# Storing the first output tile of an RMS-norm matmul in 60 and 68 rows, and the next three as one

## The chip, the cores and the metric

The kernel runs on one core of one Trainium2 chip. The metric is the device time of one execution in microseconds: 208.53 us, the median of three runs (208.49 to 208.7). Every instruction time below comes from one further execution, recorded by the hardware profiler.

## What is computed

```
x: 16 x 1024 x 512, float32     gamma: 512     weight: 512 x 768, float32
rms    = sqrt(mean(x**2, axis=-1, keepdims=True) + eps)
output = matmul(x / rms * gamma, weight)        # 16 x 1024 x 768, float32
```

## The kernel before

The 16384 rows of x are cut into 128 tiles of 128 rows (`NT`, L122). For each tile, ScalarE (ACT) squares and sums the rows (L197) and takes the root; VectorE (DVE) makes the reciprocal (L204). GpSimd (POOL) casts x to bf16 (L189, and L260 for the last four tiles of each 16). TensorE (PE) transposes the tiles two features at a time as 32-bit words (L231), and DVE copies them back (L240); the tiles of L260 are turned by DVE itself (L271). Then PE multiplies a tile with the weights in four steps of 128 features, each one product of 512 and one of 256 columns (L300). The sum in PSUM is scaled by the reciprocal root into an output buffer `ot`: even tiles by ACT (L279), odd ones by DVE (L281), in `finish_tile`. The weights are multiplied by gamma once, at the start.

No layer decides the order: the kernel writes its operations down in order, and `Order.emit` sends each to its engine with the waits that its reads and writes ask for.

Three kinds of transfers use the 16 DMA engines, from two queues:

- The queue of SyncE (SP; q1 in the profile) first gets the loads of tiles 0 to 31 and the weights: x in 4 tiles, the weights in two halves, x in 4, 8, 8 and 8 tiles. Then it gets all 22 stores of the output, each issued by SP when its last tile has been scaled.
- The queue of ACT (q10) gets gamma (512 numbers, as two rows) at the start, and later twelve loads of 8 tiles of x.

`stretches` (L128) says how the tiles of x and of the output are grouped into transfers. An output store usually covers a group of `OG` = 8 tiles; the first group has stores of 1, 1, 2 and 4 tiles, the last but one of 4 and 4, the last of 4, 2 and 2 (L139). There are four `ot` buffers of 8 tiles, used in turn. `rows` (L141) gives a transfer's place in memory: partition p of a group of t tiles holds the t rows p*t to p*t + t - 1, so that the part of a partition in a store is one stretch of memory: 3072 bytes for one tile, 6144 for two, 24576 for eight. In the first 8 tiles of the output the groups are of 4 tiles, so tiles 0, 1 to 3 and their parts lie at offsets within a stretch of 4 rows.

`store` (L288) is called after every tile and issues the transfer behind the last tile of its group. After the last one the program ends when the stores have landed.

Of the kernel before, what the change touches and what calls it, by code (L numbers as in the profile page):

```python
# [16 lines left out]
P = 128  # L17
# [83 lines left out]
def kernel(  # L101
# [9 lines left out]
    PE, DVE, ACT, POOL, SP = nc.tensor, nc.vector, nc.scalar, nc.gpsimd, nc.sync  # L111
    order = Order(tc)
# [5 lines left out]
    out = out.flatten_outer_dims()  # L118
# [5 lines left out]
    XG, OG = 16, 8  # L124
# [3 lines left out]
    def stretches(group, parts):  # L128
        first, size, i = {}, {}, 0
        for g in range(NT // group):  # L130
            for n in parts.get(g, [group]):
                for t in range(i, i + n):
                    first[t], size[t] = i, n
                i += n
        return first, size

    last = NT // OG - 1
    x_first, x_size = stretches(OG, {0: [4, 4]})
    o_first, o_size = stretches(OG, {0: [1, 1, 2, 4], last - 1: [4, 4], last: [4, 2, 2]})  # L139

    def rows(ap, i, n):  # L141
        base, t = (i - i % OG, OG) if OG <= i < XG else (x_first[i], x_size[i]) if i < OG else (i - i % XG, XG) if i < 2 * XG else (i - i % (2 * XG), 2 * XG)
        return ap[base * P:(base + t) * P, :].rearrange("(p t) d -> p t d", t=t)[:, i - base:i - base + n, :]

    def sb(name, shape, dtype):
        return nc.alloc_sbuf_tensor(name, shape, dtype).ap()
# [11 lines left out]
    ot = [sb(f"ot{n}", [P, OG, O], F32) for n in range(OTS)]  # L158
# [10 lines left out]
    def cells(name, slot, i, n=1):  # L169
        return [(name, slot, t) for t in range(i, i + n)]  # L170
# [114 lines left out]
    def accumulator():  # L285
        return next(turns) % 3

    def store(i):  # L288
        first, n = o_first[i], o_size[i]
        s = first // OG % OTS  # L290
        if i == first + n - 1:
            src = ot[s][:, first % OG:first % OG + n, :]
            order.transfer(SP, lambda: SP.dma_start(out=rows(out, first, n), in_=src), reads=cells("ot", s, first % OG, n))

    def hold(lhsT, of):
        run(PE, lambda: PE.ldweights(lhsT), of)  # L296
# [20 lines left out]
    def finish_tile(i, a, engine):  # L317
        s = i // OG % OTS

        before = [("ot", s, i % OG - 1)] if i == o_first[i] + o_size[i] - 1 else []  # L320
        scale(engine, ot[s][:, i % OG, :], ops[a][:, :O], rstd[:, i:i + 1],
              [("ops", a, 0), ("ops", a, 1), ("rstd", i)] + before, [("ot", s, i % OG)] + (opening if i == OG * (OTS - 1) else []))
        store(i)
# [158 lines left out]
```

## Time and profile before

| | |
|---|---|
| median of three runs | 208.53 us (208.49 to 208.7) |
| the profiled execution | 209.87 us |
| its span, first to last instruction | 207.9 us |
| granted PE clock, mean | 0.985 |
| moved by the DMA engines | 85.62 MB, mean 412 GB/s |
| read from / written to HBM | 35.13 MB / 50.33 MB |

How to read the lines that follow in the prediction. Of the page, the first line gives each engine's busy time, its share of the span and its instructions. The line that begins with DMA cuts the span into 40 slices of 5.2 us; each digit is the mean busy share of the 16 DMA engines in tenths. The lines that begin with q1 and q10 give the packets of a queue, its MB, and its packets' time as a share of 16 engines' span. A packet is what one engine moves in one piece; a store or load of 128 partitions makes a packet for each partition, and each engine that took part adds one of 4 bytes that raises the semaphore. The chain follows the work that ended last back from the last instruction. A line of the waits gives who waited for whom: total us, times, longest. A line of the windows gives a stretch in us, its length, the busy us of PE, weight loads, DVE, ACT and POOL with their instructions, the granted clock, the DMA share and the GB/s.

SP's issues of the first stores, from its timeline: two from 12.88 us to 14.69 (tiles 0 and 1), one at 17.20 (tiles 2 and 3), and one at 24.39 (tiles 4 to 7). The last scaling is that of tile 127 on DVE, from 197.96 for 1.02 us, and the last store is issued at 199.3.

### The profile page before, as it was taken

The numbers are of one execution on the slowest core, as the hardware profiler recorded it, in microseconds if no ns is written. First come the engines' busy times: TensorE is split into PE (matmuls) and PEld (weight loads), VectorE is DVE, ScalarE is ACT, GpSimd is POOL, SyncE is SP. The second block draws the span as 40 slices with busy tenths as digits, with TensorE's granted clock in tenths as the row PEclk, the third lists the DMA queues.
The fourth block names the chain that finished last, engine by engine and source line by source line (L and its number), as shares of the span: only waits on it lengthen the run. The fifth ranks groups of instructions, "written<-read, shape, count | busy, mean of one in ns | idle before, by whom it ended". The sixth has DMA issues, their size and how long they took to land.

```text
span 207.9 us, 2754 instructions
## 1 busy us (share of the span) xinstructions
PE 194.0 (93%) x1212; PEld 72.8 (35%) x717; DVE 149.4 (72%) x255; ACT 144.5 (70%) x343; POOL 60.0 (29%) x34
## 2 busy tenths in 40 slices
PE   7799999999999999999999999999999999999900
PEld 0244433443443334433443334443433334343300
DVE  0446557998589966998579966998579966999310
ACT  2698898877777686877777686777777686763300
POOL 1437651154206250154306060150703306000000
PEclk9999999999999999999999999999999999999995
DMA  5999999999999999999999999999999999999991
GB/s 207 426 433 448 378 418 430 421 439 418 440 419 432 429 429 435 430 427 426 435 421 421 441 427 432 432 427 418 426 440 419 440 435 424 430 423 426 421 394 58
DMA packets 5920, 85.62 MB, mean 412 GB/s; under 512 B 658, under 2 KB 660, under 8 KB 1556
## 3 DMA queue, kind: packets, MB, share of 16 engines
q1 hardware_dynamic: 4176, 60.29, 68.6%
q10 hardware_dynamic: 1732, 25.17, 28.4%
q8 instruction: 7, 0.11, 0.2%
q14 instruction: 5, 0.04, 0.0%
HBM read 35.13 MB, written 50.33 MB: 411 GB/s over the span
## 4 chain that ended last, share of the span: by engine, by line
PE 90%; DMA 2%; DVE 1%; issue 1%; ACT 1%; SPq 0%
PE ps L300 80%; PE ps L231 10%; DMA xt<-in_x_dram 2%; DVE ot L281 0%; ACT jk L197 0%; DVE xT L240 0%; DVE w_bf L281 0%; ACT ssq L202 0%; DVE rstd L204 0%; SPq L477 0%; SPq L436 0%
## 5 line engine op out<-in xcount | busy, mean ns | idle before, releaser
L300 PE MATMUL ps<-w_bf,xT 128*128 128x256 bf16 (+1 forms) x783 | 145.4, 326 | 1.1 <-DVE w_bf L281 0.2
L279 ACT ACTIVATE ot<-ps,rstd 128x768 f32<-128x768 f32 x64 | 57.6, 900 | 46.7 <-PE ps L300 46.5
L197 ACT ACTIVATE jk<-xt 128x512 bf16<-128x512 f32 x128 | 78.7, 618 | 3.1 <-DMA xt<-in_x_dram 3.1
L189 POOL CAST xb<-xt 128x2048 bf16<-128x2048 f32 (+3 forms) x21 | 46.4, 2218 | 110.0 <-DMA xt<-in_x_dram 57.6
L281 DVE TENSOR_SCALAR ot<-ps,rstd 128x768 f32<-128x768 f32 x64 | 64.8, 1013 | 9.7 <-PE ps L300 9.2
L296 PEld LDWEIGHTS <-xT 128*128 128x128 bf16 x400 | 39.3, 98 | 59.6 <-issue 58.2
L231 PE MATMUL ps<-ident_f,xb 128*128 128x128 f32 x200 | 54.4, 276 | 1.1 <-POOL xb L189 1.1
L240 DVE COPY xT<-ps 128x1024 bf16<-128x1024 bf16 (+1 forms) x53 | 34.6, 654 | 26.0 <-PE ps L231 25.2
L271 DVE STREAM_TRANSPOSE xTq<-xq 32x256 f32<-32x256 f32 x112 | 48.7, 435 | 1.9
L231 PEld LDWEIGHTS ps<-ident_f,xb 128*128 128x128 f32 x200 | 28.2, 143 | 46.4 <-issue 43.6
L300 PE MATMUL ps<-w_bf,xTq 128*128 128x256 bf16 (+1 forms) x217 | 41.8, 324 | 0.4
L197 ACT ACTIVATION_READ_ACCUMULATOR jk<-xt 128x1 f32 x128 | 24.3, 189 | 0.0
L296 PEld LDWEIGHTS <-xTq 128*128 128x128 bf16 x112 | 11.0, 98 | 14.5 <-issue 14.5
L260 POOL CAST xq<-xt 128x2048 bf16<-128x2048 f32 x7 | 13.3, 1894 | 4.2 <-DVE xTq L271 4.2
L204 DVE RECIPROCAL rstd<-ssq 128x8 f32<-128x8 f32 (+3 forms) x20 | 3.8, 192 | 7.1 <-ACT ssq L202 6.9
L202 ACT ACTIVATE ssq<-ssq,eps_sb 128x8 f32<-128x8 f32 (+3 forms) x20 | 6.0, 300 | 0.7
L300 PE MATMUL ps<-ot 128*128 128x512 bf16 x10 | 4.8, 628 | 1.4 <-DVE eps_sb L354 1.4
L279 ACT ACTIVATE w_bf<-ot,g_sb 128x768 bf16<-128x768 f32 x2 | 1.9, 936 | 1.1 <-DMA ot<-in_weight_dram 1.1
L377 DVE COPY g_sb<-ps 128x4 f32<-128x4 f32 x1 | 0.2, 161 | 3.2 <-PE ps L371 3.2
L341 ACT ACT_TABLE_LOAD x1 | 1.3, 1283 | 1.5 <-SPq L436 1.5
L281 DVE TENSOR_SCALAR w_bf<-ot,g_sb 128x512 bf16<-128x512 f32 (+2 forms) x3 | 1.4, 483 | 0.6 <-DMA ot<-in_weight_dram 0.6
L371 PEld LDWEIGHTS ps<-ident_f,ot 2*128 2x128 f32 x2 | 0.3, 200 | 2.6 <-issue 2.6
(10 smaller groups left out, 2.0 us busy)
## 6 DMA issues: line engine op xcount, KB each, us to landing
out_dram<-ot SPq DMA_DIRECT2D x13, 3072.0 KB, 22.9
xt<-in_x_dram ACTq DMA_DIRECT2D x12, 2048.0 KB, 20.0
xt<-in_x_dram SPq DMA_DIRECT2D x3, 2048.0 KB, 18.3
out_dram<-ot SPq DMA_DIRECT2D x4, 1536.0 KB, 11.9
out_dram<-ot SPq DMA_DIRECT2D x3, 768.0 KB, 8.8
xt<-in_x_dram SPq DMA_DIRECT2D x2, 1024.0 KB, 7.3
ot<-in_weight_dram SPq DMA_DIRECT2D x2, 768.0 KB, 7.0
out_dram<-ot SPq DMA_DIRECT2D x2, 384.0 KB, 21.0
```

Source lines behind the costliest of these rows:

```text
L189: run(POOL, lambda: POOL.tensor_copy(out=xb[s][:, i % 8:i % 8 + n, :], in_=src), of, cells("xb", s, i % 8, n))
L197: run(ACT, lambda: ACT.activation(out=jk[n], in_=src[:, 0, :], func=AF.Square, accum_out=ssq[:, i:i + 1]), of, [("jk", n), ("ssq", i)])
L202: run(ACT, lambda: ACT.activation(out=ssq[:, s], in_=ssq[:, s], func=AF.Sqrt, scale=1.0 / D, bias=eps_sb), [("ssq", t) for t in range(i, i ...
L204: run(DVE, lambda: DVE.reciprocal(out=rstd[:, s], in_=ssq[:, s]), [("rms", i)], [("rstd", t) for t in range(i, i + n)])
L231: run(PE, lambda: PE.transpose(out=tp[b][:, t, h, :], in_=words[:, lo:lo + P], identity=ident_f), cells("xb", s, j % 4 * 2 + t) + ["ident" ...
L240: run(DVE, lambda: DVE.tensor_copy(out=dst[:, t:t + n, :], in_=src[:, t:t + n, :]), [("tp", b)], cells("xT", j % XTS, t, n))
L260: run(POOL, lambda: POOL.tensor_copy(out=xq, in_=src), of, ["xq"])
L271: run(DVE, lambda: DVE.transpose(out=dst, in_=src), ["xq"], [("xTq", n)])
L279: run(ACT, lambda: ACT.mul(out=dst, in_=src, mul=r), reads, writes)
L281: run(DVE, lambda: DVE.tensor_single_scalar(out=dst, in_=src, scalar=r, op=mybir.AluOpType.mult), reads, writes)
L296: run(PE, lambda: PE.ldweights(lhsT), of)
L300: run(PE, lambda: PE.add_instruction(mybir.InstMatmult(name=nc.get_next_instruction_name(), engine=mybir.EngineType.PE, ins=[PE.lower_ap(r ...
```

## The change

The output's first group is stored as tile 0, tiles 1 to 3, and tiles 4 to 7. The store of tile 0 is issued as two transfers, one behind the other, of partitions 0 to 59 and 60 to 127. So there are still four transfers in the group. On the engines other than SP no instruction is added, taken away or moved.

```diff
-    o_first, o_size = stretches(OG, {0: [1, 1, 2, 4], last - 1: [4, 4], last: [4, 2, 2]})
+    o_first, o_size = stretches(OG, {0: [1, 3, 4], last - 1: [4, 4], last: [4, 2, 2]})
...
+    DIVIDED = (0,)
+    PARTS = [slice(60), slice(60, P)]
+
     def store(i):
         first, n = o_first[i], o_size[i]
         s = first // OG % OTS
         if i == first + n - 1:
-            src = ot[s][:, first % OG:first % OG + n, :]
-            order.transfer(SP, lambda: SP.dma_start(out=rows(out, first, n), in_=src), reads=cells("ot", s, first % OG, n))
+            src, dst = ot[s][:, first % OG:first % OG + n, :], rows(out, first, n)
+            for part in PARTS if first in DIVIDED else [slice(0, P)]:
+                store_rows(dst[part], src[part], cells("ot", s, first % OG, n))
+
+    def store_rows(dst, src, of):
+        order.transfer(SP, lambda: SP.dma_start(out=dst, in_=src), reads=of)
```

## The prediction

> **What bounds the kernel now.** I read the page first, then the windows of the tail, then the packet records of the trace. Two things on the page look like the bound at once:
>
> ```profile
> PE 194.0 (93%) x1212; PEld 72.8 (35%) x717; DVE 149.4 (72%) x255; ACT 144.5 (70%) x343; POOL 60.0 (29%) x34
> ...
> DMA  5999999999999999999999999999999999999991
> ...
> q1 hardware_dynamic: 4176, 60.29, 68.6%
> q10 hardware_dynamic: 1732, 25.17, 28.4%
> ...
> PE 90%; DMA 2%; DVE 1%; issue 1%; ACT 1%; SPq 0%
> ```
>
> The chain of work gives 90% to PE, but it stops where an instruction stops: at the last eviction (DVE L281, 197.96 to 198.98 us). The span runs on to 207.9. What lies between is one wait in the list of SP's own waits, beside the windows of the tail (the columns: stretch, its length, five engines, PE clock, DMA share, GB/s):
>
> ```profile
> SPq L477 <- DMA out_dram<-ot: 7.3, 1, 7.3
> ```
>
> ```profile
> 190.00:198.00 8.00, 7.87 (x49) 2.25 (x23) 3.98 (x7) 2.70 (x3) 0.00 (x0) 1.00 1.00 422
> 198.00:202.00 4.00, 0.00 (x0) 0.00 (x0) 0.98 (x1) 0.00 (x0) 0.00 (x0) 0.98 0.97 407
> 202.00:203.00 1.00, 0.00 (x0) 0.00 (x0) 0.00 (x0) 0.00 (x0) 0.00 (x0) 0.50 0.68 283
> 203.00:204.00 1.00, 0.00 (x0) 0.00 (x0) 0.00 (x0) 0.00 (x0) 0.00 (x0) 0.50 0.25 104
> 204.00:205.00 1.00, 0.00 (x0) 0.00 (x0) 0.00 (x0) 0.00 (x0) 0.00 (x0) 0.50 0.19 80
> 205.00:206.00 1.00, 0.00 (x0) 0.00 (x0) 0.00 (x0) 0.00 (x0) 0.00 (x0) 0.50 0.10 43
> 206.00:207.00 1.00, 0.00 (x0) 0.00 (x0) 0.00 (x0) 0.00 (x0) 0.00 (x0) 0.50 0.03 12
> ```
>
> The reader is to see that the 16 DMA engines are full to about 202 us and then do not stop together: a share of 0.19 is three engines of 16, and 0.10 is 1.6. The packet records (start, duration, bytes and queue; no engine number) say how. In a backlog each packet starts 3 to 4 ns before the previous one on its engine ends, and store and load packets alternate while both queues have work, so the 16 sequences can be strung together again. From 3.5 to 192 us no engine has an idle stretch that matters. The last store lands on 13 engines between 202.2 and 203.6 us, on two at 205.36 and 205.45, and on the last at 206.68. I call these three Z, Y and X. X, Y and Z are never short of packets; five of the quick engines are, for 0.04 to 0.63 us at 194.7, waiting for the next store. So the end is the work of one DMA engine, added up from the start of the run, and PE is not late for it: the last store is issued at 199.3, and X begins its first packet of it only at 204.82.
>
> **The change, part by part.** The number of stores stays 22, and SP's issues too (0.33 us each). Tile 0 goes out at the same place, behind the x loads in the same queue, whose packets last until 26.1 us on the first engine that gets through them, so its second issue (14.4 us at the latest) is covered by 11 us. The store of tiles 1 to 3 takes the place of the old one of tiles 2 and 3, issued at 17.20, covered by 9 us; tile 1 leaves at 17.20 and not at 14.4, into a queue that has not come to it. No wait is added that anything stands behind, and SP computes nothing. The output buffers are reused four groups later and the waits show no engine waiting for a store before the end. Loads alternate with stores packet by packet whatever is behind them, so a longer store queue does not hold them back. Should they land 1.5 us later all the same, the casts have room: the last one that waits for a load (POOL L189, 171.42 us) and the one behind it end at 175.2, and PE turns those tiles some 12 tiles of 1.46 us before its end, at about 180. PE's idle time for POOL is 1.1 us, all in the opening. So PE's time is left as it is, and the sum is one over packets.
>
> *The merge.* Per engine, 8 packets of 3072 B (121 ns) and 8 of 6144 B (234 ns) become 8 of 9216 B. That size is not in the trace; between 6144 B and 12288 B (460 ns) the line gives 347 ns, an estimate. With the 3.4 ns of overlap: 8 x (0.118 + 0.231) - 8 x 0.344 = 0.04 us less on each engine.
>
> *The split.* What counts is how many engines a store of 60 rows and one of 68 rows use. The packet counts bear on it. On q1, 29 transfers of 128 rows made 4176 packets, 144 each: 128 rows and 16 semaphore writes, one for each engine, 8 rows on each. On q10, 12 loads of 144 leave 4 of 1732: the gamma load of two rows, two rows and two semaphore writes, so two engines. Both are equal shares on the most engines that allow them. For 60 rows that is 15 engines with 4 rows, for 68 rows 4 engines with 17, since no larger number up to 16 divides 68. The bounds from the nearest rows: shared as evenly as 128 rows are, 68 rows cost nothing extra (0 us); on two engines like gamma they are 34 rows each, with the 4 of the other store 30 more than the 8 of now, 3.5 us on those. I take 17, the division that both rows obey. Then four engines carry 21 rows of tile 0 and not 8: 13 x 0.118 = +1.53 us; eleven carry 4: 4 x 0.118 = -0.47 us; one carries none: -0.94 us. With the merge and a semaphore write of 6 ns saved: +1.49, -0.51 and -0.99 us. (Were the one that sits out 60 rows among the four, it would have +1.0 in place of +1.49, which changes no case below.)
>
> The Trainium skill ("DMA: Bandwidth & Descriptors", Why a DMA increments its semaphore by 16 and not by 1) states that division as the rule and adds that such a DMA takes the lowest-numbered engines; the packet counts above agree with the first half, and no record here numbers an engine.
>
> *Where it ends.* Nothing idles on X, Y and Z after tile 0's packets (26 to 34 us), so what they gain or lose there reaches the end whole. If none of the three is among the four, X ends at 206.68 - 0.51 = 206.17, the four at 203.6 + 1.49 = 205.1 at most, and Y at 204.9: the run is 0.51 us shorter. Its span would be 207.4 of 207.9, its own time 209.36 of 209.87; the median of the runs shown, 208.53, becomes 208.02.
>
> **The rivals.**
>
> *X gets 17 rows.* The place is X's store queue at 26 to 34 us, the price 1.49 us, and it decides from the ninth row of tile 0 that X gets: with 21 it is 206.68 + 1.49, median 210.02, slower. Four of 16 engines make it 0.25 by count. Against it: in the opening eight engines start their first x packet at 1.95 to 2.04 us and eight at 2.64 to 2.77, and X is most likely of the second eight; if the order follows the numbers on which two rows and four rows also start, X is far from the four. For it: the slow stretch of the opening makes engines fall in step, which leaves X's start uncertain, and the first loads on q10 reach the engines in another order each time, so order proves little.
>
> *Z or Y gets them.* 205.36 or 205.45 + 1.49 = 206.85 or 206.94 takes X's place: +0.17 to +0.26 us, median 208.75. By count 0.36 (0.39 is left for the forecast). Z is the third engine to start in the first eight, which speaks for this case; the size is so small that a packet or two that took longer carries it over the bound.
>
> *The idle one is X.* Then X gains 0.99 and ends at 205.69, later than Y's 204.9 and the four's 205.1: median 207.54. By count one in 16, or one in 12 of those that are not the four. The Trainium skill (same page, Latency and other measured facts) says that engines 7 and 15 are usually slower than the rest; here three are, by 2 to 4 us, and if 15 is X this is its case.
>
> *The split moves nothing.* If 60 and 68 rows spread over 16 engines as evenly as they can, every engine has 7 to 9 rows of tile 0 and 16 more semaphore writes of 6 ns: 0.04 us saved, within 0.12 us either way, median 208.5. The packet counts speak against it. The Trainium skill (same page, Rules for kernel authors) advises against two transfers to disjoint partition halves, since both spray over all 16 engines; by it this rival holds.
>
> **How the numbers follow.** X in the four 0.23; Z or Y in the four 0.25, below its count because the two cases that follow the forecast get more than theirs; neither, with X at four rows, 0.32; X the idle one 0.15, above its count because the one engine that ends alone is the one most likely to differ in kind; nothing moved 0.05. The likeliest is 208.0 us, with 207.5 to 208.2 as its own range together with the idle one. Leaving X's case out would leave 0.23 out, so the range goes from 207.4 (0.99 gained and 0.1 for packets that vary) to 210.1. A measurement of this kernel tells about 0.2% (0.4 us) from no change. Faster by more: 0.29 of the forecast's 0.32 and all of the idle one's 0.15, 0.44. Slower by more: 0.23 and 0.11 of Z's and Y's, 0.34. Within: 0.22.
>
> **What would show it.** q1 should have 4176 - 3 x 144 + 75 + 72 + 144 = 4035 packets; 4176 would mean even shares. The first packets of the tile 0 stores should last longer on four engines than on the rest. SP's last wait should go from 7.3 to 6.8 us with the last DVE eviction still at 198.0; if the eviction moves too, PE was touched, and I was wrong that loads are not. In the tail the share after 204 us should fall, and the four loaded engines show between 203.7 and 205.1. If one of them ends after 206.5, a rival with 1.49 us has it.

## The result, and the profile after

The first set of runs, seven of each kernel, gave 209.99 us for the changed kernel and 208.70 for the one before: a ratio of 1.005, interval 1.0031 to 1.007, so 0.5% slower where 0.24% faster was forecast. Five further sets on other occasions gave 1.0016 (0.9997 to 1.0034), 0.9989 (0.9965 to 1.0013), 1.0012 (0.9986 to 1.0037), 1.0002 (0.9975 to 1.0029) and 1.0029 (0.9986 to 1.0071). The mean of the six is 1.0016, with 0.0009 as its standard error from their scatter: an interval of about -0.06 to +0.39%. So the change is not faster by what was forecast; it is slower by a little, or not at all. Executions more than 1.5% above the lowest of their kernel are left out of the ratios, 16 of the 67 of the changed kernel and 10 of the 140 of the one before beside it, so the ratios speak for the rest alone. Of those that count, 12 of 51 of the changed kernel took 210 us or more, and 13 of 130 of the one before; the medians are 209.04 and 208.96.

The profiled execution of the changed kernel took 208.78 us, the lowest of its set, and the span is 206.8. These are the lines of its page that stand where those of before stood:

```profile
PE 193.9 (94%) x1212; PEld 72.9 (35%) x717; DVE 149.4 (72%) x255; ACT 144.9 (70%) x343; POOL 60.2 (29%) x34
...
DMA  6999999999999999999999999999999999999992
...
q1 hardware_dynamic: 4035, 60.29, 69.0%
q10 hardware_dynamic: 1732, 25.17, 28.5%
...
PE 91%; DMA 2%; DVE 1%; issue 1%; ACT 1%; SPq 0%
```

PE does the same work in the same time; the packets of q1 are 4035, as worked out for shares of 15 x 4 and 4 x 17. (The prediction's 4176 for even shares is a slip; they make 4176 - 3 x 144 + 2 x 80 + 144 = 4048.) Its DMA issues show the two parts and the merged store as their own rows, with KB each and, where known, us to landing:

```profile
out_dram<-ot SPq DMA_DIRECT2D x1, 1152.0 KB, 25.4
out_dram<-ot SPq DMA_DIRECT2D x1, 204.0 KB
out_dram<-ot SPq DMA_DIRECT2D x1, 180.0 KB
```

The tail: SP's last wait, and the windows with the DMA share in the last column but one.

```profile
SPq L484 <- DMA out_dram<-ot: 6.1, 1, 6.1
```

```profile
198.00:202.00 4.00, 0.00 (x0) 0.00 (x0) 1.02 (x1) 0.00 (x0) 0.00 (x0) 0.98 0.99 416
202.00:203.00 1.00, 0.00 (x0) 0.00 (x0) 0.00 (x0) 0.00 (x0) 0.00 (x0) 0.50 0.69 289
203.00:204.00 1.00, 0.00 (x0) 0.00 (x0) 0.00 (x0) 0.00 (x0) 0.00 (x0) 0.50 0.22 92
204.00:205.00 1.00, 0.00 (x0) 0.00 (x0) 0.00 (x0) 0.00 (x0) 0.00 (x0) 0.50 0.15 61
205.00:206.00 1.00, 0.00 (x0) 0.00 (x0) 0.00 (x0) 0.00 (x0) 0.00 (x0) 0.50 0.04 18
```

The wait is 1.2 us shorter than in the profile of before (7.3), with the last eviction at 198.03 and not 197.96. Read alone, this pair of profiles would say that the change saves a microsecond. The set says the opposite: these are single draws of a tail that differs from one execution to the next.

Stringing the packets together as before, and now reading each engine's share from its packets of 3072 bytes, gives when the last store landed on the engines, and how many rows of tile 0 they had:

```
execution                    the quick engines     the late ones (rows of tile 0)
before (209.87)              13: 202.2 to 203.6    205.36 Z (8)   205.45 Y (8)    206.68 X (8)
before, again (209.02)       11: 202.8 to 203.8    204.13 to 205.09, four of them (8)   205.52 Z (8)
changed, 1st set (208.78)    13: 202.2 to 203.3    204.61 (21)    205.38 Z (4)    205.56 (21)
changed, 2nd set (210.98)    10: 203.1 to 203.2    204.38 (21)    204.82 Z (4)    205.21 (21)    205.41 (4)    205.66 (21)    207.74 (21)
changed, 3rd set (210.21)    12: 202.0 to 203.2    204.00 (4)     204.58 (21)     205.48 Z (4)    206.81 (21)
changed, 4th set (210.04)    12: 203.0 to 203.6    205.03 (21)    205.09 Z (4)    205.23 (21)     206.81 (21)
changed, 5th set (210.68)    7: 202.9 to 203.7     204.31 to 205.38, five of them (4; Z 204.76)   204.82 (21)   205.43 (21)   206.07 (21)   207.43 (21)
changed, 6th set (210.01)    10: 202.6 to 203.2    203.86 (21)    204.12 (4)      204.90 Z (4)    205.11 (21)    206.45 (21)    206.71 (21)
```

In all six of the changed kernel, four engines had 21 rows, eleven 4 and one none. The packet of 9216 bytes took 347 ns, the value estimated. Z is known by its pattern: in the before profile 136 of its 204 packets between 45 and 190 us took 8 to 60 ns longer than the usual 611 or 912, and such an engine is there in every profile that could be strung together, with 4 rows in the changed kernel. X and Y are not there again: they were slow in that one execution, through 18 and 14 packets that took up to 0.5 us longer. What ends last in the changed kernel is in all six one of the four with 21 rows, and in the first four sets the same engine. It can be known again too: it brings in three pieces of 8 KB of instructions (at about 29 to 33, 93 and 152 us), and in the two profiles of before it had ended among the quick ones, at 202.85 and 202.93. One warning goes with this: five of the six profiled executions took 210.0 us or more, which only 12 of the 51 did, so they show what ends a long execution and not the usual one.

### The profile page after: what moved, and what is told of

The parts are those of the page before. It is cut to its first block, busy times and chain, and to the rows that moved or that the text cites. A ratio compares the mean times of both kernels' runs of the same rounds, so it can differ in the third digit from the quotient of the medians.

```text
span 206.8 us, 2753 instructions
## 1 busy us (share of the span) xinstructions
PE 193.9 (94%) x1212; PEld 72.9 (35%) x717; DVE 149.4 (72%) x255; ACT 144.9 (70%) x343; POOL 60.2 (29%) x34
## 3 DMA queue, kind: packets, MB, share of 16 engines
q1 hardware_dynamic: 4035, 60.29, 69.0%
## 4 chain that ended last, share of the span: by engine, by line
PE 91%; DMA 2%; DVE 1%; issue 1%; ACT 1%; SPq 0%
PE ps L307 80%; PE ps L231 10%; DMA xt<-in_x_dram 2%; DVE ot L281 0%; ACT jk L197 0%; DVE xT L240 0%; DVE w_bf L281 0%; ACT ssq L202 0%; DVE rstd L204 0%; SPq L484 0%; SPq L443 0%
```

## The experiments

Theories before them: **U**, four engines have lost 1.5 us of their room, so what befalls them shows at the end; **M** or **C**, the merge or the second store of tile 0 costs by itself; **N** or **V**, sets of runs scatter and the kernels do not differ. **F** was formed after the first four experiments: an engine that is late loses more on the stores that follow. Each set stands beside runs of the kernel before on the same chip. All edits are to the changed kernel unless said.

### The change again, its parts, and a larger dose

The changed kernel again, without an edit:

> The changed kernel once more, for a second profile and for times. Theory U (unequal rows): the four engines with 21 rows of tile 0 end 1.49 us later than the quick ones did, at 203.2 to 204.6 us, and so have only about 1 us of room left before the constantly slow engine (205.4); any packets that take longer on one of them in a run then show at the end. Expected: about 1.0 us (0.3 to 0.7%) slower than before in the median, with more spread from run to run than before, and a profile whose last engine is one with 21 rows, or the constantly slow one if the four were spared. Rival M (merge or one more cut): slower by a constant 1 us, all engines alike. Rival N (noise of the chip): equal to before within 0.2%.

Measured: 1.0016 (0.9997 to 1.0034), a third of the first set's, under U's 0.3% and inside N's 0.2%. Its executions, between 208.51 and 210.98 us, are spread more widely than the 26 of before (208.49 to 209.91), as U says; in a later set those of before go up to 211.63.

The merge alone, tile 0 in one store:

```diff
-    DIVIDED = (0,)
+    DIVIDED = ()
```

> Tile 0 as one store of 128 rows, tiles 1 to 3 as one store. Theory U: every engine has 8 rows of tile 0, so equal to before or 0.04 us faster, within 0.2%. Rival M, if the merge is what costs: about 1 us slower, like the changed kernel. Rival N: equal to before.

Measured: 1.001 (0.999 to 1.003). The merge costs nothing that can be told. Its profile has Z at 205.55, and an engine with the usual 8 rows last, at 206.05, with 3.4 us of longer packets: late engines of X's kind come without any cut.

An even cut:

```diff
-    PARTS = [slice(60), slice(60, P)]
+    PARTS = [slice(64), slice(64, P)]
```

> As the changed kernel, but tile 0 cut into 64 and 64 rows, which 16 engines divide into 4 and 4. Theory U: packets on the first queue 4176 (no fewer than before), equal to before within 0.2%. Rival M, if the cut of tile 0 is what costs: about 1 us slower. Rival N: equal.

Measured: 1.0055 (1.0026 to 1.0084), 1.2 us in the mean, which U does not give and M does, with 4048 packets (the 4176 of the expectation is the slip named above). In its profile Z and two others end together, at 206.3, all with the usual 8 rows. It was run again below.

The larger dose:

```diff
-    PARTS = [slice(60), slice(60, P)]
+    PARTS = [slice(124), slice(124, P)]
```

> As the changed kernel, but tile 0 cut into 124 and 4 rows. 124 is 4 x 31, so by equal shares four engines get 31 + 1 rows, 24 more than before, and twelve get none. Theory U: packets 4176 - 3 x 144 + 128 + 144 + 2 x 4 = 4024; the four end 24 x 0.118 - 0.04 = 2.8 us later than they did, at 205.3 to 206.4 us without delays, so that one of them is last in nearly every run: 0.5 to 2.5 us slower than before, likeliest 1.7, and slower than the changed kernel by up to 1.3. Rival M: as the changed kernel, no more. Rival N: equal to before.

Measured: 1.019 (1.0145 to 1.0235), 4.0 us slower in the mean, above the 2.5 us that was the upper end. The packets are 4024, as expected. The wait and the windows of its tail:

```profile
SPq L484 <- DMA out_dram<-ot: 9.4, 1, 9.4
```

```profile
203.00:204.00 1.00, 0.00 (x0) 0.00 (x0) 0.00 (x0) 0.00 (x0) 0.00 (x0) 0.50 0.27 117
204.00:205.00 1.00, 0.00 (x0) 0.00 (x0) 0.00 (x0) 0.00 (x0) 0.00 (x0) 0.50 0.26 111
205.00:206.00 1.00, 0.00 (x0) 0.00 (x0) 0.00 (x0) 0.00 (x0) 0.00 (x0) 0.50 0.28 117
206.00:207.00 1.00, 0.00 (x0) 0.00 (x0) 0.00 (x0) 0.00 (x0) 0.00 (x0) 0.50 0.24 98
207.00:208.00 1.00, 0.00 (x0) 0.00 (x0) 0.00 (x0) 0.00 (x0) 0.00 (x0) 0.50 0.19 80
208.00:209.00 1.00, 0.00 (x0) 0.00 (x0) 0.00 (x0) 0.00 (x0) 0.00 (x0) 0.50 0.04 18
```

A share of 0.25 is four engines of 16, and it stands at that for four microseconds: the reader sees the four loaded engines work alone. Their packets say that they had 32 rows each and landed at 207.6, 207.8, 207.9 and 208.7, where the rows alone add 2.8 us to the 202.2 to 203.6 of quick engines before. The rest is longer packets: those over 60 ns longer than usual add 2.2 to 3.8 us on each of the four after 45 us, and 0 to 0.5 us on the seven quickest. Of 40 last packets of a store on the four between 45 and 165 us, 72% took over 60 ns longer than usual; of the 100 on ten other engines (Z and one whose packets mix with Z's left aside) 6%.

### The other part alone, the even cut again, another share

```diff
-    o_first, o_size = stretches(OG, {0: [1, 3, 4], last - 1: [4, 4], last: [4, 2, 2]})
+    o_first, o_size = stretches(OG, {0: [1, 1, 2, 4], last - 1: [4, 4], last: [4, 2, 2]})
```

> Tile 0 in 60 and 68 rows, tile 1 and tiles 2 and 3 stored apart as before. Theory U (four engines with 21 rows of tile 0 in place of 8 have 1.5 us less room): 0.15 to 0.6% slower than before, like the changed kernel, and packets 4176 - 144 + 75 + 72 = 4179. Theory M (some part of the merge costs): equal to before within 0.15%.

Measured: 1.001 (0.9989 to 1.0031), packets 4179. The middle is inside M's 0.15%, and the interval reaches well into U's range, so it does not decide between them.

> The even cut once more: 64 and 64 rows, then tiles 1 to 3. Its first runs were 0.55% slower (0.26 to 0.84), which theory U does not give. Theory U with variation between sets of runs (V): within 0.25% of before this time. Theory C (a second store for tile 0 costs by itself, whatever its shares): 0.4 to 0.7% slower again, and then the 60 and 68 rows add nothing that can be told from it.

Measured: 1.0016 (0.9987 to 1.0045). The middle lies under C's 0.4%, but the interval reaches 0.45%. Sets of a dozen runs of one kernel differ by 0.4%. The two sets of the even cut together stand at 0.36%, above the 0.16% of the changed kernel, though no engine has more rows than another: that a second store of tile 0 costs something by itself is not excluded. The last engine of its second profile, at 206.60, again had the usual 8 rows.

```diff
-    PARTS = [slice(60), slice(60, P)]
+    PARTS = [slice(100), slice(100, P)]
```

> Tile 0 in 100 and 28 rows, then tiles 1 to 3. 100 is 10 x 10 and 28 is 14 x 2, so by equal shares ten engines get 12 rows, four get 2 and two get none; packets 4176 - 432 + 110 + 42 + 144 = 4040. Theory U: ten engines are 4 x 0.118 - 0.04 = 0.43 us later, six 0.75 to 0.99 us earlier; within 0.2% of before if the constantly slow engine is of the ten (+0.4 us at most), up to 0.4% faster if it is of the six. Theory C: 0.4 to 0.7% slower. Its profile also tells from the rows which group the constantly slow engine is in.

Measured: 1.003 (1.0004 to 1.0055), packets 4040. In its profile Z has 12 rows, so it is of the ten, and lands at 205.79. The ratio is above U's 0.2%; the plain difference of the two means, 0.3 us, is within the 0.4 us that U gives for this. The interval does not part U from C.

> The changed kernel a third time, in one set with the two cuts. Theories U and C: 0.2 to 0.6% slower than before, with a wider spread than before. Theory V alone (sets of runs differ, the kernels do not): within 0.15%.

Measured: 0.9989 (0.9965 to 1.0013), outside U's range; V holds here. The lowest executions were 208.26, 208.32 and 208.37; those of before have not been under 208.48 in any set.

### Before against itself, two sets of one kernel, and the dose moved to the end

> The kernel before, put against itself: what a set of runs of one kernel tells at all. Theory V (a set of a dozen runs of one and the same kernel stands some tenths of a per cent off another set): the ratio may be off 1 by up to 0.3%. If it is within 0.1%, the first result of 0.5% is no scatter of sets.

Measured: 1.0006 (0.9978 to 1.0033). By the expectation's own rule this speaks against scatter of sets behind the first 0.5%; but the interval alone is a quarter of a per cent to either side, and the sets of the changed kernel itself lie from -0.11 to 0.5%. Its profile, the second of before, has the last landing at 205.52:

```profile
SPq L477 <- DMA out_dram<-ot: 5.7, 1, 5.7
```

> The changed kernel a fourth time. Its three sets so far stood at 0.5, 0.16 and -0.11%. Theory U with V: between -0.15 and 0.5%, about 0.2% slower on the mean of all sets, and in its profile one of the four engines with 21 rows, or the constantly slow engine, ends last.

> The same kernel a fifth time, in the same set as the fourth, on the same chip. Theory V: it differs from the fourth by more than 0.15% in the mean of the runs, though nothing differs between the two. If the sets differ by chip alone, it equals the fourth within 0.1%.

Measured: 1.0012 (0.9986 to 1.0037) and 1.0002 (0.9975 to 1.0029): on one chip the two sets agree within 0.1%, which speaks for chips or occasions more than for sets, but cannot settle it. In both profiles one of the four with 21 rows ends last, as the fourth's expectation has it.

The dose of 124 and 4 rows, with the opening as in before, on tile 112:

```diff
-    o_first, o_size = stretches(OG, {0: [1, 3, 4], last - 1: [4, 4], last: [4, 2, 2]})
+    o_first, o_size = stretches(OG, {0: [1, 1, 2, 4], last - 1: [1, 3, 4], last: [4, 2, 2]})
...
-    DIVIDED = (0,)
-    PARTS = [slice(60), slice(60, P)]
+    DIVIDED = (NT - 2 * OG,)
+    PARTS = [slice(124), slice(124, P)]
```

> The opening stored as in the kernel before; instead tile 112, the first of the last but one group, is cut into 124 and 4 rows, and tiles 113 to 115 are one store. The four engines get the same 24 rows more as in the run with 124 and 4 rows of tile 0 (3.9 us slower), but at about 185 us, when the last load of x has landed. Theory F (an engine that is late loses more at the end of each of the ten stores that come while loads are under way): only the 2.8 us of the rows are left, so the four end at 203.2 + 2.8 = 206.0 to 206.4 us and the run is 0.3 to 1.2 us slower than before. Plain sum (all of the 3.9 us is from the rows): 3 to 4.5 us slower, as with tile 0.

Measured: 1.0064 (1.0037 to 1.0091), 1.3 us slower in place of 4.0 with the same rows. SP's last wait and the tail:

```profile
SPq L484 <- DMA out_dram<-ot: 6.4, 1, 6.4
```

```profile
203.00:204.00 1.00, 0.00 (x0) 0.00 (x0) 0.00 (x0) 0.00 (x0) 0.00 (x0) 0.91 0.48 197
204.00:205.00 1.00, 0.00 (x0) 0.00 (x0) 0.00 (x0) 0.00 (x0) 0.00 (x0) 0.50 0.41 172
205.00:206.00 1.00, 0.00 (x0) 0.00 (x0) 0.00 (x0) 0.00 (x0) 0.00 (x0) 0.50 0.16 68
206.00:207.00 1.00, 0.00 (x0) 0.00 (x0) 0.00 (x0) 0.00 (x0) 0.00 (x0) 0.50 0.06 25
```

The four end at 205.3, 205.4, 206.4 and 206.7 us in an execution whose quick engines ended at 203.1 to 203.3; the loaded engines end 2.2 to 3.6 us behind the quick ones, and 5.4 to 6.5 with the early cut. So about two thirds of what the early dose costs is not its rows; by its one profile it is what the late engines lose afterwards. Theory F holds here in kind; the 1.3 us and the last landing are just above what it gave (1.2 us and 206.4).

### The same rows late, a dose between, and the change a sixth time

The late cut with 60 and 68 rows, in two sets (`PARTS` as in the change, the rest as in the late dose):

> The opening stored as before; tile 112 cut into 60 and 68 rows, tiles 113 to 115 one store. The same 13 rows more on four engines as in the changed kernel, but at about 185 us. Theory F: the loaded engines end 1.5 us later than they would, at 203.7 to 205.0 us, and lose nothing further, so they are seldom last; the others end 0.5 us earlier: between 0.3% faster and equal, and its lowest runs 0.2 to 0.5 us under the 208.5 that before does not go below. Theory V: within 0.15%, and the lowest runs at 208.5.

> The same kernel once more, so that the scatter of sets is seen beside it: within 0.3% of the other set of it, with its lowest runs at the same time within 0.15 us if these are set by the constantly slow engine and not by chance.

Measured: 1.0026 (0.9995 to 1.0056) and 1.0014 (0.9981 to 1.0046), with lowest executions at 208.40 and 208.47. F's gain did not come. In the profile of the first the last engine, at 208.31, had no extra rows but 5.4 us of longer packets after 45 us, and the four ended at 206.3 to 207.2, later than F has them, with 2.5 to 3.8 us of longer packets each; in that of the second the four landed at 203.5 to 205.0, as F says, and no engine after 205.0. One execution of a kernel has the tail forecast, another has not.

```diff
-    PARTS = [slice(60), slice(60, P)]
+    PARTS = [slice(92), slice(92, P)]
```

> Tile 0 in 92 and 36 rows, then tiles 1 to 3. By equal shares 92 is 4 x 23 and 36 is 12 x 3: four engines get 26 rows, 18 more than before. Rows alone: the four end 2.1 us later, at 204.3 to 205.6, so 0 to 0.2 us slower than before. Theory F: they lose 1 to 3 us more on the stores that follow, so 1.0 to 3.0 us slower, between the 0.3 of the changed kernel's sets and the 4.0 of the 124 and 4 rows.

Measured: 1.0048 (1.0014 to 1.0081), 1.0 us in the mean, at the lower edge of F; 4032 packets. In its profile the four (26 rows) landed at 204.8 to 206.2; their last packets were longer in only 30% of the cases, no more often than on other engines in this execution.

> The changed kernel a sixth time, beside the late cut. Five sets so far differ from before by 1.17, 0.51, -0.48, 0.19 and 0.02 us in the mean. Expected between -0.3 and 0.8 us, with lowest runs at 208.3, under before's 208.5, and highest ones over before's.

Measured: 1.0029 (0.9986 to 1.0071), 0.7 us in the mean; the lowest at 208.53, so the lower floor did not show in this set.

By dose then, in the mean against before: 0 rows 0.15 us (merge alone) and 1.2 and 0.3 us (the even cut), 13 rows 0.35 us (six sets, -0.5 to 1.2), 18 rows 1.0 us, 24 rows 4.0 us; 24 rows late 1.3 us. The early 24 rows stand clear of what 0 rows gave; 13 and 18 do not.

## Why the prediction was wrong, point by point

*What bounds the kernel.* Right: the end is the last landing of a store on one DMA engine, with PE long done. All profiles have it, with SP's last wait between 5.7 and 9.4 us. In every one that could be strung together more than one engine is late.

*The shares.* Right: 4035 packets; four engines with 21 rows, eleven with 4, one with none; and 4024, 4032, 4040 and 4048 packets for the other cuts, each equal shares on the largest number of engines that divides the rows. The Trainium skill ("DMA: Bandwidth & Descriptors", Why a DMA increments its semaphore by 16 and not by 1) states this; all five cuts agree. What the Trainium skill says of two transfers to disjoint partition halves (same page, Rules for kernel authors), that they are not worth it, agrees with the even cut too (1.0055 and 1.0016), but by the same counts a cut that divides unevenly is not such a pair.

*PE and the loads untouched.* Right as far as the pair of profiles shows: the evictions run 0.07 us later throughout, an offset that is there from tile 1 (13.37 and 13.30 us), before the first packet of tile 0.

*"Nothing idles on X, Y and Z ... so what they gain or lose there reaches the end whole" and X ends at 206.17.* This is the first step that failed. It took the order of the engines in one execution for the order of the kernel. X and Y were late by longer packets in that execution. The profiled time of before already held the warning: 209.87 us is 1.34 over the median of 208.53, and X's 206.68 less 1.34 is 205.34, Z's time. The second profile of before, 209.02 us where the median of its set is 208.99, bears this out: Z ends last, at 205.52, and no engine ends 1.3 us behind it as X did. So the usual end is no more X's; that it is mostly Z's is argued from these numbers. A gain on X is then worth nothing, and the rivals that hung on who X is were about an engine that is not there as a rule.

*"The four at 203.6 + 1.49 = 205.1 at most".* This is the second, and it takes away the gain that was left. The two of the four that can be known again by their pieces of instructions had ended at 203.06 and 202.85. For the first the sum holds in two of three profiles: 203.06 + 1.49 = 204.55, measured 204.61, 204.58 and 205.23. For the second it gives 204.34, measured 205.56, 206.81 and 206.81: 1.2 to 2.5 us of longer packets on top. In the last of the three these come before 45 us, while its extra rows are under way, in the other two mostly at the ends of the stores. The other three profiles have the first at 205.66, 205.43 and 206.71 and the second at 207.74, 206.07 and 206.45. So the room that the sum had counted on, from 205.1 to Z, was not there. The price of a row was itself at fault in half of the executions: the sum has each extra row at 0.118 us, which the 1st and 3rd sets' profiles show, but in those of the 2nd, 4th and 6th sets the rows of 3072 bytes took up to 1.4 us each on the engines with 21 of them, together 0.5 to 2.4 us more than 121 ns each on eleven of these twelve. In that of the 5th set one of the four shows it. What makes them longer there is open.

*Z with 4 rows ends 0.5 us earlier.* Nearly so: 205.38, 204.82, 205.48, 205.09, 204.76 and 204.90, in the mean 205.07, against 205.36 and 205.52; its own longer packets vary by as much. The lowest executions fell in three of six sets to 208.26, 208.32 and 208.35, where before never went under 208.48: that may be the forecast's gain, at half its size, in executions in which nothing befalls the four, but none of those was profiled. In the six that were, one of the four ends last.

*The rivals.* "Z or Y gets 17 rows" had nearly the measured size (+0.17 to 0.26 us), but not for its reason: Z had 4 rows in all six profiles. The rival that was missing is the one that happened: a quick engine among the four ends after Z. By the prediction's last sign, one of the four after 206.5 us, a rival with 1.49 us would have it; five profiles show that sign, and none of the engines is Z; those of four had ended among the quick ones before. Nor do extra rows alone make an engine late: in the merge alone and the two even cuts the last engines have 8 rows and end at 206.05 to 206.60, after or beside Z. The range, 207.4 to 210.1, held the medians of all six sets, taken over the executions that the ratios count (208.78 to 210.01), and being so wide it tells little; the sign did not hold.

*What stays open.* Why a packet takes longer on some engines in some executions, and whether lateness causes it or goes with it. Where an engine was more than 3 us behind the middle one, the last packet of a store was longer in 72% of the cases with the early dose, against 6% elsewhere; in the changed kernel in 60% and 80% against 0 and 6% in two profiles, but in none in that of the 4th set, and in that of the 5th on most engines with 4 rows too; with 92 and 36 rows in 30% against 29%. The early and late doses show that the same rows cost more when they come early; they do not show how. And whether the change costs its 0.16%, or nothing, and if it costs, whether by its uneven rows or by the second store: with sets that scatter by 0.2% each, six do not settle it. The first set's 0.5% was at the edge of that scatter.

## What to carry to other kernels

Where DMA engines are full from start to end, the end is a maximum over 16 sums, and a store that leaves some engines with more rows takes from their room, not from an average: ask for every engine what it would need to become the last, the quick ones too. Before a profile's tail is moved about by half a microsecond, compare its own time with the runs: when it is 1.3 us above the median, its last engine is not the typical one. A forecast under 0.3% on such a kernel is below what one set of a dozen runs can tell, whichever way it comes out.

## What the runs showed of the hardware

A store of 68 rows ran on four engines with 17 rows each, one of 124 rows on four with 31, one of 60 on fifteen; only 128, and 64, filled all 16. An engine with store and load packets waiting takes them in turn, one packet each, whether a packet has 4 bytes or 24576. Packets of 24576 bytes took 912 ns, but on some engines, and on different ones from one execution to the next, the last packet of a store took up to 0.6 us more. One engine in nearly every profile had over half of its packets 8 to 60 ns longer, some 3.3 to 3.7 us over the run, and ended 1.3 to 3.7 us behind the quickest. Instructions came in as seven pieces of 16 KB, about every 25 us, each on another engine and 0.9 to 1.7 us long; the smaller ones of 8 KB came on two engines, and in six profiles of uneven cuts these two were among the four with the most rows.

Executions also differ in the opening: the second eviction of DVE's line, that of tile 3, started between 15.87 and 17.23 us in the first ten profiles, and the difference is still there at the last one, between 197.66 and 199.43. This is the last eviction in the profile of 100 and 28 rows, the latest of them:

```profile
199.43 1.02 DVE L281 TENSOR_SCALAR ot<-ps,rstd 128x768 f32<-128x768 f32 x1 [1.58 <-PE ps L307]
```

No row of a store has left by then in the opening, so this difference of 1.4 us is none of the change's.
